# Fetching experts head by head from the first head on, with the memory values moved under the fetches

## The chip, the cores and the metric

One core of one Trainium2 chip runs the whole program in one launch. The time is device microseconds of that core. The core has TensorE (PE), VectorE (DVE), ScalarE (ACT), GpSimd (POOL) and SyncE (SP, which here only issues DMAs), each with its own instruction queue, and 16 DMA engines.

## The reference

Two transformer blocks over 256 tokens of width 1024. Block 1: attention and retention, `w_out`, then a layer of 16384 experts of which each token takes 8 heads x 16; block 2: SSD and latent attention, attention to 256 memory tokens, a convolutional feed-forward layer. What matters here is the expert layer:

```python
q = (xb @ w_query).reshape(tb, 8, 2, 128)
s = einsum('thpd,hpnd->thpn', q, sub_keys)          # 2 x 128 scores per token and head
top_s, top_i = top_k(s, 16)
cand = top_s[:, :, 0, :, None] + top_s[:, :, 1, None, :]
best_s, pos = top_k(cand, 16);  gate = softmax(best_s)
u = expert_down[eid];  act = gelu(einsum('thkd,td->thk', u, xb))
out = einsum('thk,thkd->td', gate * act, expert_up[eid])
```

and, of memory attention in block 2, `k = mem_h @ wk` and `v = mem_h @ wv`, which depend on nothing but the memory tokens.

## The kernel before, in words

The tokens are two tiles of 128, one token per partition. All products with weights are made of three passes (`mm3`, L173 to L175) on a high and a low half: `piece` (L148) loads 512 KB of a weight (`raw`, SP), rounds it on ScalarE (`wh`, L167) and takes the rest on VectorE (`wl`, L168). The pool of these tiles has three buffers of each.

Block 1 (`mix1`) runs attention (`diff_*`), retention (`ret_*`), scaling, transposes (`to_T`, L223) and `w_out`. Between its steps `fill(n)` draws pieces of work from a generator, to keep TensorE busy while other engines work: first the projections `rqk`, `rv`, `rg`, then `memory_values`, that is eight pieces of `w_mem_v` and eight of `w_mem_k`, whose results go to DRAM (`memkv`). What is left over after block 1 is handed on as `self.memory`.

`queries` (L606) multiplies by 16 pieces of `w_query`, two per head, and makes the scores `sS` of four (head, half) pairs at a time. `picks` and `choose` (L631) find the 16 best of 128, twice, and the 16 best sums, for four heads of one tile at once, so four units in all; every step is on VectorE, and the generators yield an estimate of their cost, by which `picking` spreads them over other work. The first unit is done while the queries are still running.

`experts` (L688) then goes through 2 tiles x 128 slots. A slot is one indirect DMA (L767, GpSimd's queue) that brings for each of the 128 tokens one row of 8 KB, 1 MB in all, into one of eight buffers `uv`: 1024 numbers of `expert_down` and 1024 of `expert_up`. VectorE takes the dot product with the normed token (`junk`, L770, result in `dots`), ScalarE the gelu of a pair of slots (L773), VectorE writes for each slot a diagonal matrix of gate times gelu (`dg`, L779), and TensorE multiplies the diagonal with the second half of the row and sums all slots of a tile in PSUM (L783, four rows in the trace per slot). The next fetch into that buffer waits for these. Under tile 0 run the other units of the choice and the memory values left over; between the tiles `joined` adds the sum to the residual `xr`. Block 2 follows.

The order on each engine is that of the program text, as far as a scheduler in the compiler doesn't interleave the independent strands.

Of the kernel before, what the change touches and what calls it, by code (L numbers as in the profile page):

```python
# [8 lines left out]
F32 = mybir.dt.float32  # L9
# [105 lines left out]
class K:  # L115
    def __init__(self, tc, I, out, dbg):
        self.tc, self.nc, self.I, self.out, self.dbg = tc, tc.nc, I, out, dbg


# [28 lines left out]
    def piece(self, src, shape, between=None):  # L148
# [3 lines left out]
        def t(tag, dt):  # L152
            x = self.wp.tile([128, 1024], dt, name=tag, tag=tag)
# [8 lines left out]
        for i in range(shape[0] if between else 1):  # L162
# [5 lines left out]
            self.wl = nc.vector.tensor_sub(lo[:, s], raw[:, s], h[:, s])  # L168
# [140 lines left out]
    def mix1(self):  # L309
# [3 lines left out]
        with self.tc.tile_pool(name="m1", bufs=1, reuse_waits="tile") as mp:  # L313
# [184 lines left out]
            fill(2)  # L498
            a = diff_turn(p)
            p = diff_scores(2)  # L500
            w = ret_scores(0)
# [3 lines left out]
            ret_out(0, w)  # L505
            w = ret_scores(1)
            fill(1)
# [4 lines left out]
            ret_out(1, w)  # L512
            w = ret_scores(2)
            fill(2)
            a = diff_turn(p)
            ret_out(2, w)
            w = ret_scores(3)
# [10 lines left out]
            fill(2)  # L528
            self.to_T([blk(h) for h in range(4)], [dg] * 4, mT[0], mT[1], 0)
            fill(2)  # L530
# [22 lines left out]
            fill(1)  # L553
# [6 lines left out]
            self.memory = fill  # L560
# [47 lines left out]
    def queries(self, pool, skT, sS):  # L608
# [4 lines left out]
        for b in range(16):  # L613
            if b < 2:
                o = two[b]
            else:
                o = self.pa([128, 256])
                self.proj_T(self.hT, self.piece(I["w_query"][b], [8, 128]), 8, o)
            if b == 2:
                self.r = self.res_r()  # L620
            if b % 4 == 0:
                qT = pool.tile([128, 4, 256], F32, name="qT", tag="qT", bufs=2)
            nc.scalar.activation(qT[:, b % 4], o, AF.Copy)
            if b % 4 == 3:
                q = b // 4
                for t in range(2):
                    s = self.pb([128, 4, 128])
                    for i in range(4):
                        nc.tensor.matmul(s[:, i], qT[:, i, t * 128:(t + 1) * 128], skT[:, 4 * q + i],
                                         start=True, stop=True)  # L630
                    nc.scalar.activation(sS[t][q], s, AF.Copy, scale=self.r[:, t:t + 1])  # L631
            yield

    def choose(self, t, hf, vals, idx, P):

        nc = self.nc
        H = 4
        hs = slice(4 * hf, 4 * hf + 4)
# [9 lines left out]
        yield 700  # L648
        yield from self.extract([cand[:, i] for i in range(H)], [cs[:, i] for i in range(H)],
                                [best[:, i] for i in range(H)], [pos[:, i] for i in range(H)], 610)  # L650
# [7 lines left out]
        yield 450  # L658
# [13 lines left out]
        yield 900  # L672
        io = self.io16[:, None, None, :].to_broadcast([128, H, 16, 16])
        ij = P([2, H, 16], "rij")
        for s in range(2):
            eq = P([H, 16, 16], "eq", F16)
            nc.vector.tensor_tensor(eq, ab[:, s, :, :, None].to_broadcast([128, H, 16, 16]), io, op=OP.is_equal)  # L677
            yield 1130
            nc.vector.tensor_mul(eq, eq, ix[:, s, :, None, :].to_broadcast([128, H, 16, 16]))
            yield 600  # L680
# [3 lines left out]
            yield 870  # L684
# [3 lines left out]
    def experts(self):  # L688


        nc, I = self.nc, self.I
        with self.tc.tile_pool(name="p2", bufs=1, reuse_waits="tile") as p2:
# [8 lines left out]
            sS = [[P([4, 128], f"sS{t}{q}") for q in range(4)] for t in range(2)]  # L701
# [4 lines left out]
            mr = [P([4, 128], f"mr{t}") for t in range(2)]  # L706
            gf = P([1024], "gf")
            nc.sync.dma_start(gf, I["ffn_gr"].to_broadcast([128, 1024]))
            self.fg = P([1024], "fgr")
            nc.sync.dma_start(self.fg, I["final_g"].to_broadcast([128, 1024]))  # L710
            self.xg = [P([512], f"xg{t}") for t in range(2)]
            xn = [P([1024], f"xn{t}") for t in range(2)]

            def picks(t, hf):
                for q in (2 * hf, 2 * hf + 1):
                    yield from self.extract([sS[t][q][:, i] for i in range(4)], [mr[t][:, i] for i in range(4)],
                                            [vals[t][:, 4 * q + i] for i in range(4)],
                                            [idx[t][:, 4 * q + i] for i in range(4)], 810)
                yield from self.choose(t, hf, vals, idx, P)

            pick = [picks(t, hf) for t in range(2) for hf in range(2)]
            debt = [0]

            def picking(time, upto):

                debt[0] += time
                while debt[0] > 0:
                    while pick and len(pick) > 4 - upto:
                        cost = next(pick[0], None)
                        if cost is not None:  # L730
                            debt[0] -= cost
                            break
                        pick.pop(0)
                    else:
                        debt[0] = 0

            with self.tc.tile_pool(name="qp", bufs=1, reuse_waits="tile") as qp:
                skT = qp.tile([128, 16, 128], F32, name="skT")
                nc.sync.dma_start(skT, I["skT"])
                for b, _ in enumerate(self.queries(qp, skT, sS)):  # L740
                    if b == 3:
                        for t in range(2):
# [904 lines left out]
```

## Time and profile before

| | us |
|---|---|
| three runs | 1355.0, 1357.12, 1356.94 (median 1356.94) |
| profiled execution | 1354.52 |
| its span | 1352.6 |
| first fetch issued | 203.91 |
| last dot product begins | 880.62 |
| TensorE clock granted, mean | 0.981 |

The span is the time from the first instruction to the last; the stages follow each other: block 1 to 147.3, queries to 203.9, experts to 880.7, block 2 to the end. A busy share is an average over them, so the windows by stage are what counts.

### The profile page before, as it was taken

How to read it: one execution, taken by the hardware profiler on the slowest of the kernel's cores; microseconds unless marked ns; L12 is line 12 of the kernel's file. 1: busy time of each engine (PE TensorE's matmuls, PEld its weight loads, DVE VectorE, ACT ScalarE, POOL GpSimd, SP SyncE). 2: the span in 40 equal slices, each digit the busy share in tenths (PEclk: the TensorE clock that was granted, in tenths of full speed). 3: DMA queues.
4: the chain of work that ended last, by engine and by line, in shares of the span. 5: the costliest groups of instructions: out<-in, count | busy, mean ns of one | idle time of the engine just before them, and what ended most of it. 6: DMA issues, size and time to landing. Idle time of an engine off the chain costs nothing.

```text
span 1352.6 us, 16359 instructions
## 1 busy us (share of the span) xinstructions
PE 1158.9 (86%) x5430; PEld 792.1 (59%) x5430; DVE 997.2 (74%) x2334; ACT 489.1 (36%) x969; POOL 291.2 (22%) x280
## 2 busy tenths in 40 slices
PE   8999997668777777787777777789999999999996
PEld 6888996323223222332232222269997898999996
DVE  6877798997666666666656666678996886988887
ACT  6676653210000000100000000056878574755554
POOL 0010104335333334344343343210001000000001
PEclk9999998879999999999999999999999999999999
DMA  7636749899999999899999999936434364556562
GB/s 262 232 120 203 225 150 382 359 352 386 422 422 421 422 421 422 342 423 421 421 421 423 421 422 421 395 101 190 141 106 129 112 231 126 190 187 188 187 185 96
DMA packets 81655, 388.07 MB, mean 287 GB/s; under 512 B 8292, under 2 KB 10404, under 8 KB 48548
## 3 DMA queue, kind: packets, MB, share of 16 engines
q0 software_dynamic: 36864, 268.45, 48.2%
q1 hardware_dynamic: 42692, 115.96, 26.7%
q10 hardware_dynamic: 2016, 2.62, 0.5%
q8 instruction: 43, 0.70, 0.2%
q14 instruction: 40, 0.33, 0.1%
HBM read 383.86 MB, written 3.15 MB: 286 GB/s over the span
## 4 chain that ended last, share of the span: by engine, by line
PE 41%; DMA 23%; issue 13%; DVE 10%; POOL 6%; ACT 1%; POOLq 0%; DVEq 0%; ACTq 0%
DMA uv<-in_uv_dram,eid 23%; POOL uv L767 6%; PE pa L173 6%; PE pa L174 6%; PE pa L175 6%; PE pa L1476 4%; PE pb L173 4%; PE pb L174 4%; PE pb L175 4%; DVE junk L770 2%; DVE wl L168 1%; PE pb L783 1%; PE pb L1060 1%; DVE dg L779 1%; DVE eq L677 1%
## 5 line engine op out<-in xcount | busy, mean ns | idle before, releaser
L783 PE MATMUL pb<-uv,dg 128*128 128x512 f32 x1024 | 486.6, 620 | 168.5 <-DVE dg L779 160.0
L783 PEld LDWEIGHTS pb<-uv,dg 128*128 128x128 f32 x1024 | 190.3, 195 | 460.9 <-DVE dg L779 257.2
L770 DVE SCALAR_TENSOR_TENSOR junk<-uv,xn 128x1024 bf16<-128x1024 f32 x256 | 313.4, 1224 | 166.2 <-DMA uv<-in_uv_dram,eid 159.6
L767 POOL DMA_INDIRECT uv<-in_uv_dram,eid x256 | 260.4, 1017 | 431.7 <-PE pb L783 327.7
L168 DVE TENSOR_TENSOR wl<-raw,wh 128x1024 fp32r<-128x1024 f32 (+3 forms) x203 | 248.8, 1228 | 70.7 <-ACT wh L167 66.8
L167 ACT ACTIVATE wh<-raw 128x1024 fp32r<-128x1024 f32 (+3 forms) x203 | 212.1, 1047 | 196.5 <-PE pa L174 39.5
L773 ACT ACTIVATE dots<-dots,rs_y 128x2 f32<-128x2 f32 x128 | 37.8, 295 | 578.5 <-DVE junk L770 578.1
L173 PE MATMUL pb<-nTh,wh 128*128 128x256 f32 x416 | 117.7, 283 | 0.0
L174 PE MATMUL pb<-nTl,wh 128*128 128x256 f32 x416 | 117.7, 283 | 0.0
L175 PE MATMUL pb<-nTh,wl 128*128 128x256 f32 x416 | 117.4, 283 | 0.0
L779 DVE TENSOR_SCALAR dg<-cvt,dots,gate 128x128 f32<-128x128 f32 x256 | 78.0, 394 | 51.5 <-ACT dots L773 51.5
L174 PEld LDWEIGHTS pb<-nTl,wh 128*128 128x128 f32 x416 | 79.5, 191 | 1.0
L173 PEld LDWEIGHTS pb<-nTh,wh 128*128 128x128 f32 x416 | 79.5, 191 | 1.0
L175 PEld LDWEIGHTS pb<-nTh,wl 128*128 128x128 f32 x416 | 79.5, 191 | 0.0
L173 PE MATMUL pa<-nTh,wh 128*128 128x256 f32 x256 | 74.1, 289 | 0.0
L1500 POOL TENSOR_TENSOR xs<-xr,ng 128x512 f32<-128x512 f32 x4 | 5.1, 1294 | 313.9 <-DVE xr L1498 313.9
L175 PE MATMUL pa<-nTh,wl 128*128 128x256 f32 x256 | 72.5, 283 | 0.0
L174 PE MATMUL pa<-nTl,wh 128*128 128x256 f32 x256 | 72.4, 283 | 0.0
L173 PE MATMUL pa<-wh,nTh 128*128 128x512 f32 (+1 forms) x144 | 58.1, 412 | 8.2 <-ACT wh L167 7.1
L174 PE MATMUL pa<-wl,nTh 128*128 128x512 f32 (+1 forms) x144 | 57.6, 400 | 1.7 <-DVE wl L168 1.6
L175 PE MATMUL pa<-wh,nTl 128*128 128x512 f32 (+1 forms) x144 | 56.7, 394 | 0.0
L173 PEld LDWEIGHTS pa<-nTh,wh 128*128 128x128 f32 x256 | 48.9, 191 | 1.1 <-issue 1.0
(455 smaller groups left out, 1797.5 us busy)
## 6 DMA issues: line engine op xcount, KB each, us to landing
raw<-in_w_ffn_up_dram SPq DMA_DIRECT2D x44, 512.0 KB, 3.6
raw<-in_w_out_dram SPq DMA_DIRECT2D x24, 512.0 KB, 3.7
raw<-in_w_in_dram SPq DMA_DIRECT2D x23, 512.0 KB, 4.7
raw<-in_w_ffn_down_dram SPq DMA_DIRECT2D x22, 512.0 KB, 3.6
raw<-in_w_query_dram SPq DMA_DIRECT2D x16, 512.0 KB, 3.6
raw<-in_w_xbc_dram SPq DMA_DIRECT2D x16, 512.0 KB, 4.3
raw<-in_w_mem_v_dram SPq DMA_DIRECT2D x8, 512.0 KB, 4.7
raw<-in_w_mem_k_dram SPq DMA_DIRECT2D x8, 512.0 KB, 6.2
```

The source lines that it names most:

```text
L167: nc.scalar.activation(h[:, s], raw[:, s], AF.Copy)
L168: self.wl = nc.vector.tensor_sub(lo[:, s], raw[:, s], h[:, s])
L173: mm(out, a[0], b[0], start=start, stop=False)
L174: mm(out, a[0], b[1], start=False, stop=False)
L175: mm(out, a[1], b[0], start=False, stop=stop)
L677: nc.vector.tensor_tensor(eq, ab[:, s, :, :, None].to_broadcast([128, H, 16, 16]), io, op=OP.is_equal)
L767: nc.gpsimd.indirect_dma_start(x, None, I["uv"], bass.IndirectOffsetOnAxis(ap=eids[:, s + i:s + i + 1], axis=0))
L770: nc.vector.scalar_tensor_tensor(junk, x[:, :1024], 1.0, xn[t], op0=OP.mult, op1=OP.mult, accum_out=dots[:, i:i + 1])
L773: nc.scalar.activation(dots, dots, AF.Gelu, scale=self.r[:, t:t + 1])
L779: nc.vector.tensor_scalar(dg[:, i], self.ident, ds[:, i:i + 1], gates[:, s0 + i:s0 + i + 1], op0=OP.mult, op1=OP.mult)
L783: nc.tensor.matmul(acc[d], dg[:, i], rs[i][:, 1024 + 512 * d:1536 + 512 * d], start=s0 + i == 0, stop=s0 + i == 127)
L1476: nc.tensor.matmul(acc[d][t], a[x][:, t * 128:(t + 1) * 128], w[y][:, d], start=b == 0 and x + y == 0, stop=b == 21 and x == 1)
```

## The change

1. `memory_values` leaves the fillers of block 1. It is drawn piece by piece under tile 0's fetches, from slot 58 on. Some retention steps move to where its pieces stood.
2. Queries, scores and choices go head by head. Units of choice: head 0 of tile 0, head 1, then pairs of heads, then the two units of four heads of tile 1. The fetches begin when head 0 is chosen; the rest of the queries and choices runs under them.
3. The raw query tiles have a pool of their own (`qraw`, four buffers).
4. The low halves `wl` are taken on GpSimd from the third query piece to the end of the memory values.
5. Six `uv` buffers until slot 56, then eight.
6. `dg` moves to ScalarE; the gate is multiplied into `dots` before it by a small VectorE product. Of four slots one (`sl % 4 == 2`) has no `dg` and no matmul: VectorE multiplies and adds its row into `xr` (64 of 256 slots).
7. `xn` takes its gains by DMA and is multiplied in place.

```diff
...
+            pool = self.rawp if tag == "raw" and self.rawp else self.wp
+            x = pool.tile([128, 1024], dt, name=tag, tag=tag)
...
-            self.wl = nc.vector.tensor_sub(lo[:, s], raw[:, s], h[:, s])
+            self.wl = self.low_by.tensor_sub(lo[:, s], raw[:, s], h[:, s])
...
                 for name in ("rqk", "rv", "rg"):
                     yield from block(name)
-                yield from self.memory_values(*memory)
...
             diff_out(3, a)
-            ret_out(3, w)
             ds = ds.rearrange("p t h -> p (t h)")
             nc.vector.tensor_scalar(ds, ds, 1.0 / 128, EPS, op0=OP.mult, op1=OP.add)
             r = self.rsqrt(ds, 8)
+            ret_out(1, w)
+            w = ret_scores(2)
             for t in range(2):
                 for h in range(4):
                     nc.scalar.activation(mix[:, t, h * 128:(h + 1) * 128], dif[:, t, h], AF.Copy,
                                          scale=r[:, 4 * t + h:4 * t + h + 1])
-            fill(2)
+            w3 = ret_scores(3)
+            ret_out(2, w)
+            ret_out(3, w3)
+            fill.rest()
             self.to_T([blk(h) for h in range(4)], [dg] * 4, mT[0], mT[1], 0)
-            fill(2)
             vv = self.sm([128, 8], F32, "bvv", 1)
             nc.vector.tensor_scalar(vv, mv[:, :, :, 1].rearrange("p t h -> p (t h)"), EPS, None, op0=OP.add)
             rr = self.rsqrt(vv, 8)
...
             self.to_T([blk(4 + h) for h in range(4)], [self.pv("ret_g", h) for h in range(4)], mT[0], mT[1], 4)
-            fill(1)
...
-            self.memory = fill
+            self.memory = Filler(self.memory_values(*memory))
...
+        self.r = self.res_r()
+        for h in range(8):
+            qT = pool.tile([128, 2, 256], F32, name="qT", tag="qT", bufs=2)
+            for i in range(2):
+                o = two[i]
+                if h:
+                    o = self.pa([128, 256])
+                    self.proj_T(self.hT, self.piece(I["w_query"][2 * h + i], [8, 128]), 8, o)
+                nc.scalar.activation(qT[:, i], o, AF.Copy)
+                if h and not i:
+                    yield
+            for t in range(2):
+                s = self.pb([128, 2, 128])
+                for i in range(2):
+                    nc.tensor.matmul(s[:, i], qT[:, i, t * 128:(t + 1) * 128], skT[:, 2 * h + i], start=True, stop=True)
+                nc.scalar.activation(sS[t][h], s, AF.Copy, scale=self.r[:, t:t + 1])
+    def choose(self, t, h0, H, vals, idx, P):
...
+            for t in range(2):
+                nc.sync.dma_start(xn[t], I["ffn_gr"].to_broadcast([128, 1024]))
...
+            units = [(0, 0, 1), (0, 1, 1)] + [(0, h, 2) for h in (2, 4, 6)] + [(1, 0, 4), (1, 4, 4)]
...
+            uvs = [up] * 6
+            count = [0]
+
+            def fetch(t, acc):
+
+                gates = self.gate[t].rearrange("p h k -> p (h k)")
+                eids = self.eid[t].rearrange("p h k -> p (h k)")
+                last = None
+                for s in range(0, 130, 2):
+                    new = None
+                    if s < 128:
+                        rows = []
+                        dots = up.tile([128, 2], F32, name="dots", tag="dots", bufs=4)
+                        for i in range(2):
+                            pool = uvs[count[0] % len(uvs)]
+                            count[0] += 1
+                            x = pool.tile([128, 2048], F32, name="uv", tag="uv", bufs=uvs.count(pool))
+                            nc.gpsimd.indirect_dma_start(x, None, I["uv"],
+                                                         bass.IndirectOffsetOnAxis(ap=eids[:, s + i:s + i + 1], axis=0))
+                            junk = self.junk([128, 1024], "junk", BF)
+                            nc.vector.scalar_tensor_tensor(junk, x[:, :1024], 1.0, xn[t], op0=OP.mult, op1=OP.mult,
+                                                           accum_out=dots[:, i:i + 1])
+                            rows.append(x)
+                        nc.scalar.activation(dots, dots, AF.Gelu, scale=self.r[:, t:t + 1])
+                        nc.vector.tensor_mul(dots, dots, gates[:, s:s + 2])
+                        new = s, rows, dots
+                    if last:
+                        s0, rs, ds = last
+                        dg = up.tile([128, 2, 128], F32, name="dg", tag="dg", bufs=3)
+                        for i in range(2):
+                            sl = s0 + i
+                            if sl % 4 == 2:
+                                nc.vector.scalar_tensor_tensor(self.xr[:, t], rs[i][:, 1024:], ds[:, i:i + 1],
+                                                               self.xr[:, t], op0=OP.mult, op1=OP.add)
+                                continue
+                            nc.scalar.activation(dg[:, i], self.ident, AF.Copy, scale=ds[:, i:i + 1])
+                            for d in range(2):
+                                nc.tensor.matmul(acc[d], dg[:, i], rs[i][:, 1024 + 512 * d:1536 + 512 * d],
+                                                 start=sl == 0, stop=sl == 127)
+                    last = new
+                    yield s
+
+            two = lambda: [self.pb([128, 512]) for _ in range(2)]
+            with self.tc.tile_pool(name="qp", bufs=1, reuse_waits="tile") as qp:
+                skT = qp.tile([128, 16, 128], F32, name="skT")
+                nc.sync.dma_start(skT, I["skT"])
+                with self.tc.tile_pool(name="qraw", bufs=4) as self.rawp:
+                    query = Filler(self.queries(qp, skT, sS))
+                    query(1)
+                    nc.gpsimd.tensor_mul(xn[0], xn[0], self.xr[:, 0])
+                    self.low_by = nc.gpsimd
+                    query(2)
+                    picking(1e6, 0, 1)
+                    acc = two()
+                    tile0 = fetch(0, acc)
+                    for s in tile0:
+                        if s == 2:
+                            nc.gpsimd.tensor_mul(xn[1], xn[1], self.xr[:, 1])
+                        if s % 4 == 2:
+                            query(1)
+                        done = min(8, 2 + (s + 2) // 8)
+                        picking(1400, 0, done)
+                        if s in (12, 28):
+                            picking(1e6, 0, 2 if s == 12 else 4)
+                        if s == 54:
+                            break
+                    query.rest()
+                self.rawp = None
+            with self.tc.tile_pool(name="up2", bufs=1, reuse_waits="tile") as up2:
+                uvs += [up2] * 2
+                self.fg = up2.tile([128, 1024], F32, name="fgr")
+                nc.sync.dma_start(self.fg, I["final_g"].to_broadcast([128, 1024]))
+                self.xg = [up2.tile([128, 512], F32, name=f"xg{t}") for t in range(2)]
+                for s in tile0:
+                    if s % 4 == 2:
+                        self.memory(1)
+                    picking(1400, 1, 8)
+                    if s % 32 == 26:
+                        picking(1e6, 0, min(8, 2 * (s // 32) + 4))
+                self.memory.rest()
+                self.low_by = nc.vector
+                picking(1e6, 1, 8)
+                self.hT = (self.nt.tile([128, 8, 256], F32R, name="nTh", tag="nTh"),
+                           self.nt.tile([128, 8, 256], F32R, name="nTl", tag="nTl"))
+                for d in range(2):
+                    self.joined(0, d, acc[d], gg)
+                acc = two()
+                for s in fetch(1, acc):
...
...
```

The DMA queue of SP at the end of block 1, before (`w_mem_v`, `w_mem_k` are the memory values):

```order
L166 DMA raw<-in_w_mem_v_dram 128x2x512 x8
L166 DMA raw<-in_w_out_dram 128x2x512 x4
L166 DMA raw<-in_w_mem_k_dram 128x1024
L166 DMA raw<-in_w_out_dram 128x2x512 x4
L166 DMA raw<-in_w_query_dram 128x1024 x5
L699 DMA iota<-in_cv_dram 128x16
L708 DMA gf<-in_ffn_gr_dram 128x1024
L710 DMA fgr<-in_final_g_dram 128x1024
L739 DMA skT<-in_skT_dram 128x2048
L166 DMA raw<-in_w_query_dram 128x1024 x11
L166 DMA raw<-in_w_mem_k_dram 128x1024 x7
```

and of the change:

```order
L169 DMA raw<-in_w_out_dram 128x2x512 x8
L169 DMA raw<-in_w_mem_v_dram 128x2x512 x3
L695 DMA iota<-in_cv_dram 128x16
L705 DMA xn_1380<-in_ffn_gr_dram 128x1024
L705 DMA xn_1381<-in_ffn_gr_dram 128x1024
L781 DMA skT<-in_skT_dram 128x2048
L169 DMA raw<-in_w_query_dram 128x1024 x16
L807 DMA fgr<-in_final_g_dram 128x1024
L169 DMA raw<-in_w_mem_v_dram 128x2x512 x5
L169 DMA raw<-in_w_mem_k_dram 128x1024 x8
```

All `w_query` loads now stand behind three loads of the values and in one run; the others of the values come behind them.

GpSimd's queue from the normed tokens `xn` to the fetches, before:

```order
L743 TENSOR_TENSOR xn_1569<-xr,gf 128x1024
L743 TENSOR_TENSOR xn_1570<-xr,gf 128x1024
L767 DMA uv<-in_uv_dram,eid_1559 128x2048 x128
L767 DMA uv<-in_uv_dram,eid_1560 128x2048 x3
L828 TENSOR_TENSOR xg_1567<-xr,fgr 128x512
```

and of the change:

```order
L785 TENSOR_TENSOR xn_1380<-xn_1380,xr 128x1024
L793 TENSOR_TENSOR xn_1381<-xn_1381,xr 128x1024
L171 TENSOR_TENSOR wl<-raw,wh 128x1024 x5
L753 DMA uv<-in_uv_dram,eid_1376 128x2048 x16
L171 TENSOR_TENSOR wl<-raw,wh 128x1024
L753 DMA uv<-in_uv_dram,eid_1376 128x2048 x4
```

Five low halves stand ahead of the first fetch, and one more behind each four fetches after the first 16.

TensorE at the first turn of `mix` (L223, now L226), before:

```order
L174 MATMUL pa<-wl,memTh 128x512
L175 MATMUL pa<-wh,memTl 128x512
L173 MATMUL pa<-wh,memTh 128x512
L223 MATMUL pb<-cvt,mix 128x128
L174 MATMUL pa<-wl,memTh 128x512
L223 MATMUL pb<-cvt,mix 128x128 x2
L175 MATMUL pa<-wh,memTl 128x512
L223 MATMUL pb<-cvt,mix 128x128
L173 MATMUL pa<-wh,memTh 128x512
L223 MATMUL pb<-cvt,mix 128x128
```

and of the change (`rqk` and `rw` are retention's scores and weights):

```order
L178 MATMUL pb<-rqkTh,rqkTl 128x256
L176 MATMUL pb<-rqkTh 128x256
L177 MATMUL pb<-rqkTl,rqkTh 128x256
L178 MATMUL pb<-rqkTh,rqkTl 128x256
L481 MATMUL pb<-rv,rw 128x128 x8
L226 MATMUL pb<-cvt,mix 128x128 x8
L176 MATMUL pa<-wh,mTh 128x512
L177 MATMUL pa<-wl,mTh 128x512
L176 MATMUL pa<-wh,mTh 128x512
L178 MATMUL pa<-wh,mTl 128x512
```

The turn stood among matmuls of the values (`memTh`); now it stands between retention and `w_out` (`mTh`).

## Rows read from the trace of the kernel before

**Rows 1.** The page: gigabytes per second that the DMA moved, in 40 slices of 33.8 us.
```profile
GB/s 262 232 120 203 225 150 382 359 352 386 422 422 421 422 421 422 342 423 421 421 421 423 421 422 421 395 101 190 141 106 129 112 231 126 190 187 188 187 185 96
```

**Rows 2.** Stretches: length, busy time (instructions) of each engine, granted clock, DMA share, GB/s.
```profile
147.30:203.90 56.60, 55.97 (x468) 55.47 (x467) 52.71 (x217) 31.55 (x51) 6.03 (x2) 1.00 0.59 187
203.90:880.70 676.80, 506.03 (x1200) 211.62 (x1199) 454.68 (x1098) 61.24 (x167) 262.94 (x258) 0.97 0.99 405
225.00:310.00 85.00, 62.10 (x171) 29.95 (x170) 84.65 (x329) 15.90 (x28) 31.15 (x25) 0.85 0.92 359
310.00:406.60 96.60, 73.70 (x161) 28.67 (x160) 62.21 (x124) 5.91 (x20) 40.05 (x42) 1.00 1.01 418
406.60:555.00 148.40, 111.50 (x239) 43.56 (x239) 90.49 (x177) 8.57 (x29) 55.76 (x57) 0.99 1.01 421
555.00:590.00 35.00, 28.81 (x75) 13.58 (x74) 21.90 (x46) 6.83 (x22) 17.88 (x16) 0.90 0.87 346
590.00:880.70 290.70, 216.18 (x466) 84.06 (x465) 178.07 (x349) 17.14 (x58) 108.62 (x112) 0.99 1.00 416
```

**Rows 3.** TensorE groups, 60 to 147.3 us: count, busy us, mean ns, idle before.
```profile
L173 PE MATMUL pa<-wh,memTh 128*128 128x512 f32 x32 | 13.1, 410 | 0.0
```

**Rows 4.** Timeline of 109 to 117 us: start, length, engine, line, operation, count.
```profile
109.58 0.14 DVE L522 TENSOR_SCALAR dss<-dss 128x8 f32<-128x8 f32 x1
...
115.25 1.85 ACT L526 ACTIVATE mix<-mix,rs_y 128x128 f32<-128x128 f32 x6
...
115.25 0.40 PE L175 MATMUL pa<-wh,memTl 128*128 128x512 f32 x1
115.48 0.40 PE L173 MATMUL pa<-wh,memTh 128*128 128x512 f32 x1
115.72 0.30 PE L223 MATMUL pb<-cvt,mix 128*128 128x128 f32 x1
```

**Rows 5.** Timeline: the first query loads on SP, the first fetch on GpSimd.
```profile
134.16 12.22 SPq L166 DMA_DIRECT2D raw<-in_w_query_dram  x5
...
203.91 1.15 POOL L767 DMA_INDIRECT uv<-in_uv_dram,eid  x1 [43.57 <-DVE vals L602]
```

**Rows 6.** Timeline of GpSimd and VectorE, 153 to 161 us.
```profile
154.31 6.03 POOL L743 TENSOR_TENSOR xn<-xr,gf 128x1024 f32<-128x1024 f32 x2 [67.41 <-DVE rs_y L199]
...
153.50 1.23 DVE L168 TENSOR_TENSOR wl<-raw,wh 128x1024 fp32r<-128x1024 f32 x1
154.95 3.15 DVE L168 TENSOR_TENSOR wl<-raw,wh 128x1024 fp32r<-128x1024 f32 x1 [0.22 <-ACT wh L167]
```

**Rows 7.** DMA issues: KB each, median us from issue to landing.
```profile
raw<-in_w_query_dram SPq DMA_DIRECT2D x16, 512.0 KB, 3.6
...
uv<-in_uv_dram,eid POOLq DMA_INDIRECT x256, 13.0
```

**Rows 8.** Timeline of the steady loop, one pair of rows.
```profile
702.49 3.70 PE L783 MATMUL pb<-uv,dg 128*128 128x512 f32 x8 [1.35 <-DVE dg L779]
...
704.75 0.94 POOL L767 DMA_INDIRECT uv<-in_uv_dram,eid  x1 [2.36 <-PE pb L783]
```

**Rows 9.** Groups between 225 and 310 us.
```profile
L770 DVE SCALAR_TENSOR_TENSOR junk<-uv,xn 128x1024 bf16<-128x1024 f32 x25 | 30.4, 1215 | 0.0
...
L779 DVE TENSOR_SCALAR dg<-cvt,dots,gate 128x128 f32<-128x128 f32 x26 | 7.7, 344 | 0.3 <-ACT dots L773 0.3
...
L168 DVE TENSOR_TENSOR wl<-raw,wh 128x864 fp32r<-128x864 f32 (+1 forms) x5 | 5.6, 1111 | 0.0
```

**Rows 10.** Timeline of TensorE after two gaps.
```profile
255.23 1.12 PE L783 MATMUL pb<-uv,dg 128*128 128x512 f32 x2 [2.60 <-DVE dg L779]
...
282.78 2.07 PE L783 MATMUL pb<-uv,dg 128*128 128x512 f32 x2 [3.25 <-DVE dg L779]
```

**Rows 11.** Stretches at these gaps: TensorE busy, granted clock, DMA share, GB/s.
```profile
255.00:260.00 5.00, 3.70 (x8) 1.00 1.01 423
280.00:285.00 5.00, 2.22 (x3) 0.67 1.00 415
```

More of the change, by code (lines that the diff above doesn't have):

```diff
@@ L504, in mix1 @@
             diff_out(1, a)
-            ret_out(0, w)
-            w = ret_scores(1)
-            fill(1)
+            w = ret_scores(0)
             a = diff_turn(p)
@@ L612, in queries @@
         self.first_T([I["w_query"][b] for b in range(2)], two, self.pv("ffn_g", 0, 8))
[L613 to L631, printed above, removed]
+        self.r = self.res_r()
[14 more added lines that the diff above has]
+                nc.scalar.activation(sS[t][h], s, AF.Copy, scale=self.r[:, t:t + 1])
             yield
-    def choose(self, t, hf, vals, idx, P):
+    def choose(self, t, h0, H, vals, idx, P):
         nc = self.nc
-        H = 4
-        hs = slice(4 * hf, 4 * hf + 4)
+        hs = slice(h0, h0 + H)
         v = vals[t].rearrange("p (h s) k -> p h s k", s=2)[:, hs]
@@ L691, in experts @@
         nc, I = self.nc, self.I
-        with self.tc.tile_pool(name="p2", bufs=1, reuse_waits="tile") as p2:
+        with self.tc.tile_pool(name="p2", bufs=1, reuse_waits="tile") as p2, \
+                self.tc.tile_pool(name="up", bufs=1, reuse_waits="tile") as up:
             def P(shape, tag, dt=F32, bufs=1):
@@ L700, in experts @@
             nc.vector.tensor_copy(self.io16, iota)
-            sS = [[P([4, 128], f"sS{t}{q}") for q in range(4)] for t in range(2)]
+            sS = [[P([2, 128], f"sS{t}{h}") for h in range(8)] for t in range(2)]
             vals = [P([16, 16], f"vals{t}") for t in range(2)]
@@ L722, in experts, with picking @@
+            units = [(0, 0, 1), (0, 1, 1)] + [(0, h, 2) for h in (2, 4, 6)] + [(1, 0, 4), (1, 4, 4)]
+            pick = [(u, picks(*u)) for u in units]
             debt = [0]
-            def picking(time, upto):
+            def picking(time, t, h):
                 debt[0] += time
                 while debt[0] > 0:
[L728 to L732, printed above, removed]
+                    if not pick or (pick[0][0][0], pick[0][0][1] + pick[0][0][2]) > (t, h):
+                        debt[0] = 0
+                        break
+                    cost = next(pick[0][1], None)
+                    if cost is None:
@@ L733, in picking @@
                         pick.pop(0)
                     else:
[L735 to L742, printed above, removed]
-                            nc.gpsimd.tensor_mul(xn[t], self.xr[:, t], gf)
-                    if b >= 8:
-                        picking(2000, 1)
-                picking(1e6, 1)
+                        debt[0] -= cost
@@ new lines, in experts @@
+            with self.tc.tile_pool(name="up2", bufs=1, reuse_waits="tile") as up2:
[18 more added lines that the diff above has]
+                for s in fetch(1, acc):
+                    if s == 112:
+                        ws = [self.piece(I["w_latq"][k], [2, 432]) for k in range(3)]
+                    elif s == 120:
+                        A = [self.pa([128, 512]) for _ in range(2)]
+                        self.latents(ws, 0, A[0])
+                for d in range(2):
+                    self.joined(1, d, acc[d], gg)
+                self.latents(ws, 1, A[1])
+                ws.append(self.piece(I["w_latq"][3], [2, 432]))
+                for u in range(2):
+                    self.latents(ws, u, A[u], (3,))
```

106 lines of the change are left out of this document (20 added, 86 removed).

## Prediction

> **What bounds the kernel now.** I read the page's gigabytes per second first: from the seventh slice to the 26th the DMA moves 340 to 423, outside them mostly 100 to 260 [rows 1]. So the expert stage, half of the span, is the stage in which the memory system is the limit, and the windows by stage say how tight that limit is. From the first fetch (203.91, [rows 5]) to the end of the last one at 880.7 the DMA is 99% busy and moves 405 GB/s over 676.8 us, which is 274.1 MB; in its undisturbed stretch, 406.6 to 555, it moves 421 [rows 2]. At 421 the same bytes take 651 us: 25.7 us are lost, and the table shows where: 359 GB/s from 225 to 310 (85 x 62 / 421 = 12.5 us lost) and 346 from 555 to 590, the join of the two tiles (35 x 75 / 421 = 6.2). A fetched slot is 1.049 MB, 2.49 us at 421 GB/s.
>
> From 225 to 310 VectorE is the limit: 84.65 us busy of 85 [rows 2], 25 dot products of 1.215 us, 7.7 us of `dg`, 5.6 of low halves [rows 9], and the rest, some 40 us, mostly choosing. 25 slots in 85 us are 3.4 us a slot, against 2.49.
>
> Before the first fetch TensorE is the limit: 55.97 of the 56.6 us of the query stage, clock 1.00 [rows 2]. So there are three levers: the moment of the first fetch, the bytes moved after it, and the slots at which something other than the DMA sets the pace.
>
> **The change part by part.** I count from the profiled execution, 1354.5 us, of which 1352.6 are the span; the median of the runs is 1356.9, 2.4 more, and I add those at the end.
>
> *Block 1.* The memory values leave it: three groups of 32 matmuls on the value matrix (one of them in [rows 3]), which follow each other at 0.23 us [rows 4], 96 x 0.227 = 21.8 us, and one key piece, 24 matmuls of half the columns, 2.8 us: 24.6 us of TensorE. But they were cover. The sum of squares is scaled at 109.58, the scaled `mix` comes at 115.25, the transpose at 115.72 [rows 4]: 6.1 us in which TensorE had 26 or so of those matmuls to run. Now two retention heads stand there, and the last `ret_out` ends just ahead of the transposes. I take 9 us of new gaps (bounds 3, if the retention covers most of the chain, and 18, if every such chain is bare), and 3 us for the clock that falls after a gap: behind one of 2.60 us it held 1.00, behind one of 3.25 us it was 0.67 over five microseconds [rows 10, 11]. Block 1 ends 12 to 13 us earlier, near 134.5 for 147.3.
>
> *First fetch.* Before, the first query loads were issued at 134.16 [rows 5], 13 us ahead of their use. Now their buffers lie in memory that block 1 uses to its end, so the first is issued about 2.6 us after the last `w_out` matmul, lands 3.6 us later [rows 7] and is rounded in 1.1: TensorE stands some 8 us. Two pieces (2.9 us each by the row count and pitch) and head 0's scores end 17 us after block 1. Head 0's choice is about 45 short VectorE instructions; in 225 to 310 some two units of four heads cost 40 us, 5 us a head where four share an instruction, so one alone is between 5 and 20; I take 8.5, nearer the low end. On GpSimd the two products `xn` and five low halves come ahead of the fetches; the two products took 6.03 us [rows 6], so five more at 2.3 to 3.4 end at about the same time as the choice. The first fetch is at 134.5 + 26 = 160 (bounds 152 and 170), 44 us earlier.
>
> *Bytes.* After the first fetch now come 9 or 10 query pieces (5 MB; the low halves of the others stand ahead of it), 13 memory pieces (6.8) for seven before (3.7), and the writes of the values (some 1 MB more): about 283 MB for 274, 22 us at 421 GB/s.
>
> *Slots 0 to 67.* VectorE per four slots: four dots of 1.22 and, new, one 128x1024 sum. That operation isn't in the trace; the dot, same shape and two such inputs, took 1.215 [rows 9], a residual addition of half that width would make it 1.4, and I take 1.25 (at 1.4 it adds 0.15 x 64 = 10 us of VectorE, hidden wherever the DMA is late). Two gate products of 0.1 us are added, `dg` (0.3 each at its pace) goes to ScalarE, which was busy 61 us of 677 [rows 2] and covers it. Sum 6.3 us, under the DMA's 9.96. On top comes the choosing left over, about 80 us; by the order of the instructions some 6 us of it stand in slots 0 to 3, 17 in slots 4 to 31, and 58 in slots 32 to 67. So: slots 0 to 3 about 7 us beyond landing; slots 4 to 31 are DMA-bound, 28 x 2.49 + 6 x 1.24 (a query piece of 512 KB) = 77.2, and with two crowded places 82; slots 32 to 67 take VectorE 9 x 6.3 + 58 = 115 for a DMA need of 97.
>
> *Low halves on GpSimd.* 26 of them now run between fetches. In the trace a low half on VectorE took 3.15 us beside the product `xn` on GpSimd, 1.23 just ahead of it, and the GpSimd product 3.0 [rows 6]. So each can hold VectorE for 1.9 us. Where the DMA is the limit that is hidden; the nine in slots 32 to 67 are not: 0 to 9 x 3.0 = 27 us, nearest row 17, and I take 10, as VectorE's many small operations there have one large input or less. The Trainium skill ("SBUF — State Buffer", the section on SBUF's two separate sides) says that VectorE and GpSimd share a port pair as an exclusive lock, held for the whole instruction, for a VectorE operation with two SBUF inputs against a GpSimd operation that reads SBUF, and that the loser fully blocks. The trace agrees (3.15 for 1.23); by the rule alone every dot that meets a low half waits for its end, and the sum would lose the 27.
>
> Slots 0 to 67 then take 7 + 82 + 115 + 10 = 214 us, and slot 68 stands near 374, before 406.6. Slots 68 to 127 are DMA-bound: 60 x 2.49 = 149.4, 13 pieces 16, writes 5: 171 us, end of tile 0 at 545 for 555. In that stage GpSimd's own queue isn't late: four issues of about 1 us and a low half of 3 in 10 us.
>
> *Six buffers.* With eight, a fetch lands 13.0 us after its issue [rows 7], most of it waiting behind others; TensorE's four rows and the issue of the next fetch into a buffer 2.26 us after their start [rows 8] close the loop. Six buffers give 6 x 2.49 = 15 us per turn. That is just enough by these rows (5.5 us for the least landing, 4 for the pair's second dot and gelu, 4.5 to the reissue); above it each microsecond costs a sixth per slot. I take nothing beyond the 4 us above; bounds 0 and 0.9 us a slot, which is what 225 to 310 showed over the 2.49.
>
> *Tile 1, join and the rest.* 6.3 us of VectorE and 12 matmul rows of 0.43 (5.2 us) per 9.96 us of DMA: as before, 325.7 us [rows 2]. All told 10 us earlier: 1344.5, against the median 1347.
>
> **Rivals.** (a) *The DMA never waits:* the choosing and the locks fit between the landings, so from the first landing on the stage lasts 283 MB / 421 = 672 us and the 6 of the join. For it: 418 GB/s from 310 to 406.6 with VectorE 62 of 96.6 busy [rows 2]. Against it: 225 to 310. It ends at 160 + 7 + 678 = 845 for 880.7: 1319 profiled, 1321 as a median.
>
> (b) *Slower: the early slots go at VectorE's and the ring's pace.* Place: slots 0 to 67; mechanism: six buffers, choosing and the held port pair make each slot cost 3.4 us, as in 225 to 310 [rows 2, 9]. 7 + 68 x 3.4 = 238 us, slot 68 at 398, tile 0 ends at 569: 14 later, 1368 profiled, 1371. It decides from 3.2 us a slot on (160 + 7 + 68 x 3.2 = 384, 10 over mine). For it: that stretch had eight buffers and still lost. Against: per four slots VectorE has less to do than there.
>
> (c) *The clock.* With one row in four off TensorE, its gaps in the steady loop alternate near 1.5 and 3.3 us, and 3.25 is where the clock fell [rows 10, 11]. At half clock 12 rows take 10.3 us against 9.96: up to 0.34 x 32 = 11 us in a tile, which eats the gain: 1357. Against: at that pace the gaps close, and the clock comes back.
>
> (d) *Block 1 gains nothing:* every chain is bare; it ends at 141, the gain is 3 to 4 us: 1353.
>
> **How the numbers follow.** Chances: my forecast (gain of 4 to 20 us) 0.44, (a) 0.18, (b) 0.24, (c) 0.08, (d) 0.06. The likeliest is 1347, its own range 1337 to 1353. A measurement here can tell 0.2%, 2.7 us. Faster: the forecast, (a) and most of (d) less the cases near zero, 0.62; same 0.10 from the edges of forecast and (c), (d); slower 0.28, (b) and part of (c). From 1321, the whole of (a), to 1366, most of (b): 8 in 10.
>
> **What would show it.** The first fetch between 152 and 170 and the last `w_out` matmul near 134; slots 4 to 31 at 2.8 to 3.0 us each with the DMA above 0.95, slots 32 to 67 at 3.2 to 3.5 with VectorE over 0.95; dots of 2 to 4 us beside low halves on GpSimd; slot 68 between 365 and 385; tile 1 at 2.49 a slot with TensorE about 52% busy at clock 1.00. A first fetch after 175, slots 4 to 31 above 3.3 with a VectorE that idles (the ring), or a granted clock below 0.9 in tile 1 would prove me wrong.

## The result, and the profile after

The changed kernel takes 1389.6 us (median of 4 runs, 1387.2 to 1397.7) against 1356.0: a ratio of 1.026, 95% interval 1.022 to 1.030. It is slower, where 1347 and "faster" were forecast. The profiled execution took 1397.7, the longest of the four; its span is 1395.8.

The page, TensorE's granted clock in tenths and gigabytes per second, 40 slices of 34.9 us:

```profile
PEclk9999878888778989988889888999999999999998
...
GB/s 254 232 93 136 207 382 359 299 307 294 287 328 347 411 405 399 422 342 421 421 422 421 422 421 420 423 201 177 146 128 103 109 226 145 176 194 184 184 185 100
```

Against [rows 1] the transfers begin one slice earlier, but the slices from the eighth to the 13th show 287 to 347 GB/s, where before they showed 352 to 422. Six stretches (length, busy time of PE, PEld, DVE, ACT, POOL, then clock, DMA share, GB/s): from just behind block 1 to the first fetch, slots 0 to 31, slots 32 to 67, slots 68 to 127, the join, tile 1.

```profile
139.60:170.00 30.40, 22.83 (x170) 22.41 (x170) 20.61 (x87) 15.38 (x26) 15.49 (x8) 0.83 0.64 207
170.00:284.10 114.10, 80.79 (x270) 44.55 (x269) 83.20 (x250) 29.25 (x67) 55.55 (x43) 0.82 0.90 345
284.10:424.60 140.50, 86.78 (x240) 44.60 (x239) 127.63 (x448) 35.08 (x71) 60.34 (x43) 0.78 0.79 296
424.60:597.00 172.40, 134.90 (x438) 74.03 (x438) 122.73 (x166) 43.13 (x99) 100.18 (x69) 0.89 1.00 404
597.00:640.00 43.00, 31.88 (x72) 13.89 (x70) 28.26 (x52) 11.01 (x34) 22.28 (x19) 0.85 0.88 356
640.00:923.40 283.40, 188.66 (x339) 72.98 (x340) 182.59 (x311) 47.90 (x142) 130.46 (x110) 0.88 1.00 417
```

To be read against [rows 2]. The DMA share is 0.90 and 0.79 in the first 68 slots, and VectorE busy 127.6 of 140.5 us in the second stretch. Tile 1 moves its bytes at 417 GB/s as before, with TensorE at a clock of 0.88. The stages in us, from the starts of dot products and fetches:

| | forecast | measured | kernel before |
|---|---|---|---|
| last `w_out` matmul | 134.5 | 138.2 | 147.3 |
| first fetch | 160 | 170.0 | 203.9 |
| slot 4 | 167 | 187.1 | 230.0 |
| slots 4 to 31, each | 2.9 | 3.46 | 3.13 |
| slots 32 to 67, each | 3.5 | 3.90 | 2.47 |
| slot 68 | 374 | 424.6 | 406.7 |
| slots 68 to 127, together | 171 | 172.4 | 148.3 |
| last dot product | 870 | 923.4 | 880.6 |

The start, in a timeline of TensorE, SP and GpSimd (start, length, idle before and its releaser), which answers to [rows 4, 5]:

```profile
87.75 0.58 PE L427 MATMUL pb<-dkTh,dqTh 64*128 64x256 f32 x1 [4.47 <-ACT mix L461]
...
109.91 2.53 PE L226 MATMUL pb<-cvt,mix 128*128 128x128 f32 x8 [3.16 <-ACT mix L523]
...
146.73 0.58 PE L176 MATMUL pa<-nTh,wh 128*128 128x256 f32 x1 [7.10 <-ACT wh L170]
...
139.84 3.13 SPq L169 DMA_DIRECT2D raw<-in_w_query_dram  x4
...
169.99 1.14 POOL L753 DMA_INDIRECT uv<-in_uv_dram,eid  x1 [2.86 <-DVE eid L679]
```

Block 1 has two bare gaps, 4.47 and 3.16 us; the query loads go out at 139.84, and TensorE stands 7.10 us. Then a low half on GpSimd (297.63) and VectorE beside it, which answers to [rows 6]:

```profile
297.63 2.38 POOL L171 TENSOR_TENSOR wl<-raw,wh 128x1024 fp32r<-128x1024 f32 x1
...
297.15 3.42 DVE L671 TENSOR_TENSOR eq<-rab,io 128x512 f16<-128x512 f16 x1
300.49 0.15 DVE L760 TENSOR_TENSOR dots<-dots,gate 128x2 f32<-128x2 f32 x1
```

An `eq` product that elsewhere takes 0.70 us ends half a microsecond after the low half. The groups of VectorE between 170 and 424.6 show what was held:

```profile
L756 DVE SCALAR_TENSOR_TENSOR junk<-uv,xn 128x1024 bf16<-128x1024 f32 x68 | 90.0, 1323 | 9.8 <-DMA uv<-in_uv_dram,eid 9.5
...
L659 DVE TENSOR_SCALAR rg<-rf 128x32 f32<-128x32 f32 x3 | 3.3, 1085 | 0.0
...
L659 DVE TENSOR_SCALAR rg<-rf 128x64 f32<-128x64 f32 x2 | 0.4, 184 | 0.0
```

The dots are at 1.32 for 1.215 [rows 9]. And a one-input operation on 32 numbers per token (`rg`) has a mean of 1.085 us in one form and 0.184 in a wider one, as one of its three took 2.93 beside the low half at 236.75: being small or having one input did not spare it. The searches of the choice were spared. They ran beside low halves at their usual 0.28 us:

```profile
155.18 4.76 POOL L171 TENSOR_TENSOR wl<-raw,wh 128x1024 fp32r<-128x1024 f32 x2 [3.39 <-ACT wh L170]
...
158.89 0.28 DVE L597 MATCH_REPLACE8 mr<-vals,sS 128x128 f32<-128x128 f32 x1
```

Over the whole tile I compared each VectorE instruction that overlaps one of the 25 low halves after the first fetch with the median of its own kind: 19 of the 25 met one, most of them lost 2.0 to 2.9 us, 48.4 in all: 7.7 in slots 4 to 31, 13.9 in 32 to 67, 26.8 behind. VectorE's waits in the first 68 slots (in total, times, longest):

```profile
DVE vals L591 <- ACT sS L626: 22.7, 6, 6.0
DVE dots L760 <- ACT dots L759: 9.8, 16, 4.4
DVE junk L756 <- DMA uv<-in_uv_dram,eid: 9.5, 8, 2.3
```

The first is new: VectorE stands 22.7 us at the first maximum of a choice, for scores that come late. What holds them up stands in TensorE's longest wait over the same stretch, and in the lines around VectorE's longest single one:

```profile
PE pb L773 <- ACT dg L771: 82.7, 22, 8.4
...
328.52 2.39 POOL L171 TENSOR_TENSOR wl<-raw,wh 128x1024 fp32r<-128x1024 f32 x1
...
335.69 5.40 PE L773 MATMUL pb<-uv,dg 128*128 128x512 f32 x8 [3.61 <-ACT dg L771]
340.52 0.69 PE L178 MATMUL pa<-nTh,wl 128*128 128x256 f32 x1
...
345.47 0.49 DVE L591 MAX8 vals<-sS 128x8 f32<-128x128 f32 x2 [6.02 <-ACT sS L626]
345.88 1.21 DVE L756 SCALAR_TENSOR_TENSOR junk<-uv,xn 128x1024 bf16<-128x1024 f32 x1
```

A low half stands in GpSimd's queue behind every four fetches, and in TensorE's queue the products of a query piece stand among the rows of the slots in the same way. No wait of TensorE in these slots is put down to a low half. The low half ends at 330.91; the pass that reads it (L178) begins at 340.52, behind eight rows that waited for `dg`, and for the other pieces after the first fetch that distance is 4 to 15 us. So VectorE stands for scores, the scores wait for slot rows ahead of them in TensorE's queue, and those rows for `dg`, which comes from VectorE's dots. The last query product ends at 343.7.

### The profile page after: what moved, and what is told of

The parts are those of the page before. It is cut to its first block, busy times and chain, and to the rows that moved or that the text cites. A ratio compares the mean times of both kernels' runs of the same rounds, so it can differ in the third digit from the quotient of the medians.

```text
span 1395.8 us, 15825 instructions
## 1 busy us (share of the span) xinstructions
PE 1125.7 (81%) x5174; PEld 780.7 (56%) x5174; DVE 1044.9 (75%) x2321; ACT 565.8 (41%) x1176; POOL 409.2 (29%) x310
## 4 chain that ended last, share of the span: by engine, by line
PE 42%; DVE 19%; issue 13%; DMA 9%; POOL 8%; ACT 3%; POOLq 0%; ACTq 0%; DVEq 0%
DMA uv<-in_uv_dram,eid 8%; POOL uv L753 7%; DVE junk L756 7%; PE pb L773 6%; PE pa L176 5%; PE pa L177 5%; PE pa L178 5%; PE pa L1504 4%; PE pb L176 4%; PE pb L177 4%; PE pb L178 4%; DVE dots L760 2%; DVE xr L768 1%; DVE eq L671 1%; PE pb L1088 1%
## 5 line engine op out<-in xcount | busy, mean ns | idle before, releaser
L773 PE MATMUL pb<-uv,dg 128*128 128x512 f32 x768 | 446.9, 734 | 224.8 <-ACT dg L771 224.8
L773 PEld LDWEIGHTS pb<-uv,dg 128*128 128x128 f32 x768 | 170.3, 233 | 470.0 <-ACT dg L771 288.8
L756 DVE SCALAR_TENSOR_TENSOR junk<-uv,xn 128x1024 bf16<-128x1024 f32 x256 | 331.6, 1295 | 106.6 <-DMA uv<-in_uv_dram,eid 105.1
L753 POOL DMA_INDIRECT uv<-in_uv_dram,eid x256 | 305.3, 1193 | 361.8 <-PE pb L773 220.8
L171 DVE TENSOR_TENSOR wl<-raw,wh 128x1024 fp32r<-128x1024 f32 (+3 forms) x173 | 210.3, 1219 | 72.9 <-ACT wh L170 72.3
L178 PE MATMUL pb<-nTh,wl 128*128 128x256 f32 x416 | 117.4, 283 | 0.0
L771 ACT ACTIVATE dg<-cvt,dots 128x128 f32<-128x128 f32 x192 | 70.1, 396 | 71.2 <-DVE dots L760 71.2
L760 DVE TENSOR_TENSOR dots<-dots,gate 128x2 f32<-128x2 f32 x128 | 40.8, 318 | 71.7 <-ACT dots L759 71.7
L768 DVE SCALAR_TENSOR_TENSOR xr<-uv,dots,xr 128x1024 f32<-128x1024 f32 x64 | 85.0, 1328 | 2.0
L178 PEld LDWEIGHTS pb<-nTh,wl 128*128 128x128 f32 x416 | 79.5, 191 | 0.0
L178 PE MATMUL pa<-nTh,wl 128*128 128x256 f32 x256 | 77.2, 301 | 0.5 <-DVE wl L171 0.5
L171 POOL TENSOR_TENSOR wl<-raw,wh 128x1024 fp32r<-128x1024 f32 x30 | 73.0, 2436 | 12.5 <-ACT wh L170 12.0
```

Source lines behind the costliest of these rows:

```text
L171: self.wl = self.low_by.tensor_sub(lo[:, s], raw[:, s], h[:, s])
L178: mm(out, a[1], b[0], start=False, stop=stop)
L753: nc.gpsimd.indirect_dma_start(x, None, I["uv"], bass.IndirectOffsetOnAxis(ap=eids[:, s + i:s + i + 1], axis=0))
L756: nc.vector.scalar_tensor_tensor(junk, x[:, :1024], 1.0, xn[t], op0=OP.mult, op1=OP.mult, accum_out=dots[:, i:i + 1])
L760: nc.vector.tensor_mul(dots, dots, gates[:, s:s + 2])
L768: nc.vector.scalar_tensor_tensor(self.xr[:, t], rs[i][:, 1024:], ds[:, i:i + 1], self.xr[:, t], op0=OP.mult, op1=OP.add)
```

## The experiments

All times are medians; each kernel's runs stand beside runs of the kernel before, whose medians were 1354.8 to 1357.3.

**Low halves on VectorE.** `-  self.low_by = nc.gpsimd` (the line taken out).

> The change with all low halves on VectorE again (none on GpSimd). Theory 'ring' (six buffers, each held longer than 15 us, set the pace of slots 0 to 67): the low halves add 26 x 1.2 us to VectorE and free GpSimd's queue, slots 0 to 67 stay at 3.5 to 3.8 us, time within 8 us of the change's 1389.6. Theory 'lock' (GpSimd's low halves hold VectorE, 3.42 us for an eq product of 0.70): slots 0 to 67 fall to 3.3 us or less, 20 us or more faster (1370 or less).

1360.9 (1359.0 to 1364.1): 28.7 us less, by far the largest of the single edits. But slots 4 to 67 did not fall to 3.3 us: they took 3.65 (4 to 31) and 3.37 (32 to 67). They hold more work: with the engine of the low halves as the only edit, the last query product ends at 237.3 us for 343.7, and the memory values are done by slot 54 for 120. Slot 68 comes 8.1 us earlier; most of the gain sits in slots 68 to 127 (2.48 us each for 2.92). It needed splitting, below.

**Query tiles in the common pool; then eight buffers.** `-  with self.tc.tile_pool(name="qraw", bufs=4) as self.rawp:`; and `-  uvs = [up] * 6  +  uvs = [up] * 8`.

> The change with the raw query tiles in the common pool of three instead of their own four that reuse block 1's memory; still six uv buffers. Both theories of the fetch stage: the pace of slots 0 to 67 stays near 3.66 us. Only the first query loads go out before the end of block 1, so TensorE's 7.1 us stand after the last w_out matmul shrinks to 1 to 2 us, the first fetch comes at 163 to 165 for 170, and the time falls by 4 to 7 us.

> As e2_no_qraw, and the memory that is freed holds two more uv buffers: eight from the first fetch on. Theory 'ring': slots 4 to 31 go from 3.46 us to 2.8 or less, slots 32 to 67 from 3.9 to 3.4 (VectorE-bound), 25 to 40 us faster than e2_no_qraw. Theory 'lock' or VectorE's load alone: less than 10 us faster than e2_no_qraw, as the buffers would only wait longer for VectorE.

1385.0 and 1376.4 (1371.6 to 1385.9). The first removes TensorE's 7.1 us and has head 0's scores 4 us earlier (153.6 for 157.9), yet the first fetch is at 170.6: the choice takes 16.5 us for 12.0, beside four low halves and a product on GpSimd. The earlier fetch that I expected failed. The second gains 8.6, with 2.85 us in slots 4 to 31 (3.06 without) and 3.86 in slots 32 to 67: less than theory "ring" said, and not where the time is. The two ratios, 1.020 to 1.023 and 1.012 to 1.022, overlap, so the 8.6 is barely clear of noise.

**Six buffers in the kernel before.** `-  bufs=8  +  bufs=6` at L766.

> The kernel before with six uv buffers instead of eight, nothing else. Theory 'ring': the stretch with choosing (225 to 310) gets slower than 3.4 us a slot, and even the undisturbed slots of tile 1 rise over 2.49, 15 to 40 us slower in all. Theory 'lock': six buffers suffice for a turn of 15 us, less than 8 us slower.

1367.9, 13 us slower, a ratio of 1.010 (1.008 to 1.012), between what the two theories expect. Landing time, and tile 1:

```profile
uv<-in_uv_dram,eid POOLq DMA_INDIRECT x256, 8.6
...
600.00:892.00 292.00, 216.67 (x463) 84.49 (x463) 177.54 (x348) 17.14 (x58) 113.23 (x113) 0.99 1.00 415
```

A fetch lands after 8.6 us for 13.0 [rows 7]: two buffers less are mostly, as I read it, less waiting behind others; 2.52 us a slot in tile 1 for 2.48.

**Both, and all slots on TensorE.** e1 and e3 together; then also `-  if sl % 4 == 2:  +  if sl < 0:`.

> e3_ring8 (eight buffers, query tiles in the common pool) and e1_low_on_dve (low halves on VectorE) together. If the ring's and the lock's costs add, 1389.6 - 28.7 - 13.2 = 1347.7. If both are one cost (a buffer is held long because VectorE is held), the second edit adds little to the first: 1355 to 1361.

> e6_ring8_low_dve with every slot on TensorE again (no row summed on VectorE). VectorE loses 64 x 1.33 = 85 us, some 45 of them in tile 0, where slots 4 to 67 were VectorE-bound: theory 'VectorE's load sets the pace there' expects 10 to 25 us less than e6. Theory 'TensorE at half clock sets it' expects no gain or a loss, since TensorE gets a third more rows, unless the clock stays up.

1364.4 and 1358.9. With the low halves on VectorE, eight buffers and the common pool gain nothing (3.5 us more than e1, above both expectations). So I read the ring's 8.6 us as a consequence: buffers were kept long because VectorE was late. Taking the sums off VectorE gains 5.5, less than the 10 to 25 expected.

**All slots on TensorE in the change itself.** The same edit alone.

> The change with every slot on TensorE again (the 64 sums on VectorE undone), low halves still on GpSimd, six buffers. Theory 'lock and VectorE's load': VectorE loses 85 us, 22 of them in slots 0 to 67, and one large two-input operation in five that a low half can stop: 10 to 25 us faster than 1389.6. Theory 'TensorE's clock': its gaps shrink by a third more rows, the granted clock returns from 0.88 to 0.97 or more in tile 1, where the DMA is the limit, and nothing is gained there; a gain, if any, comes before slot 68.

1383.7, 5.9 less, under the 10 to 25 of its first theory. Tile 1 (columns as above):

```profile
620.00:906.00 286.00, 213.00 (x461) 82.92 (x462) 151.09 (x287) 56.53 (x172) 104.42 (x110) 1.00 1.01 419
```

Its clock is 1.00 for 0.88, and a slot takes 2.47 us for 2.49: the fallen clock was real, and together with the sums on VectorE, which the same edit takes away, it cost tile 1 some 2 us.

**Held without data: a product, and a memset.** e1 plus one GpSimd instruction behind every fourth fetch of tile 0: `+  nc.gpsimd.tensor_sub(scr, xn[0], hist[-4][:, 0:1].to_broadcast([128, 1024]))`, or `+  nc.gpsimd.memset(scr, 0.0)` with a ScalarE copy of one column that paces it.

> e1_low_on_dve (all low halves on VectorE) with 30 added GpSimd products of 128x1024 that nobody needs, one behind every fourth fetch of tile 0, of data that are ready by then. Theory 'lock': each holds VectorE's two-input operations and, 2.4 us long, gives back most of what e1 had gained: 15 to 30 us slower than e1's 1360.9, with VectorE operations of 2 to 4 us beside them. Theory 'order' (e1 gained because the memory values no longer stand in the queue of fetches): within 6 us of e1.

> As e7_dummy_tt, but the 30 added GpSimd instructions are memsets of the same 128x1024 tile, which read nothing. If the lock needs a GpSimd operation that reads the on-chip memory, as the skill says, VectorE keeps its pace and the time stays within 5 us of e1's 1360.9, a memset's own length in GpSimd's queue apart; if any long GpSimd instruction delays the fetches or VectorE, it comes out like e7_dummy_tt.

1379.6 and 1368.0. GpSimd's added instruction and VectorE's dots, of the product, then of the memset (count, busy, mean ns, idle before):

```profile
L779 POOL TENSOR_TENSOR scr<-xn,dots 128x1024 bf16<-128x1024 f32 x29 | 56.8, 1959 | 0.8 <-issue 0.2
...
L758 DVE SCALAR_TENSOR_TENSOR junk<-uv,xn 128x1024 bf16<-128x1024 f32 x121 | 170.4, 1408 | 32.2 <-DMA uv<-in_uv_dram,eid 31.7
```

```profile
L779 POOL MEMSET scr<- 128x1024 bf16 x29 | 28.0, 964 | 6.5 <-ACT tiny L780 6.5
...
L758 DVE SCALAR_TENSOR_TENSOR junk<-uv,xn 128x1024 bf16<-128x1024 f32 x126 | 154.0, 1222 | 58.5 <-DMA uv<-in_uv_dram,eid 58.4
```

Beside products the dots take 1.41 us, beside memsets 1.22, as alone. VectorE lost 43.6 us to the 30 products and 0.2 to the memsets by the count used above. That shows the hold, and that a product holds VectorE where a memset does not; that the reading makes the difference is likely but not separated from the length (1.96 us for 0.96). In the kernel with products VectorE has no wait for scores, so a hold alone does not make that wait. The memset kernel is 7.2 us slower than e1 all the same, where 5 were expected besides the memset's own length; its place in GpSimd's queue and the copy on ScalarE are candidates, which I did not separate.

**GpSimd for the queries only, or for the memory values only.** `self.low_by` set back, or set, at slot 56.

> The change with GpSimd's low halves for the query pieces alone; those of the memory values are on VectorE. Of the 28.7 us by which e1_low_on_dve is under the change, theory 'lock' (a held VectorE costs where VectorE sets the pace, before slot 68) puts most on the query pieces: 1375 to 1385 here. Theory 'order' (the memory values, tied to GpSimd's queue of fetches, come late and their bytes fall into the DMA-bound slots 68 to 127) puts it on the memory pieces: 1360 to 1370 here.

> The other half: GpSimd's low halves for the memory values alone, those of the queries on VectorE. Theory 'lock': 1362 to 1372, with slots 4 to 67 as in e1_low_on_dve. Theory 'order': 1378 to 1390, with slots 68 to 127 at 2.8 us or more, as in the change.

1374.9 and 1371.1: the queries' low halves cost 14.0 over e1, the memory values' 10.2. By the times both runs lie at or in the ranges of theory "lock". But the 14.0 us are not the hold alone: in e12 VectorE lost 13.0 us to its nine low halves by the count used above and waited 15.4 us for scores. And slots 68 to 127 of e13 take 2.92 us each, as theory "order" said. In e13 slots 0 to 31, 32 to 67 and 68 to 127, and VectorE's waits to slot 68:

```profile
170.80:291.00 120.20, 85.12 (x368) 53.16 (x367) 113.95 (x476) 43.63 (x86) 40.73 (x35) 0.89 0.85 324
291.00:396.40 105.40, 68.93 (x131) 29.03 (x130) 89.58 (x218) 19.90 (x50) 57.41 (x41) 0.83 0.95 376
396.40:568.60 172.20, 136.46 (x440) 74.92 (x439) 122.97 (x165) 42.83 (x99) 103.14 (x70) 0.88 1.02 417
```

```profile
DVE junk L756 <- DMA uv<-in_uv_dram,eid: 17.0, 18, 3.1
DVE dots L760 <- ACT dots L759: 4.4, 12, 0.4
```

No wait for scores is left (the last query product ends at 239.5), and slot 68 comes at 396.4 for 424.6, though VectorE does eight low halves itself. These two traces are 29 us apart and the medians 18.5, so a part of the 28 belongs to the execution that was profiled. In slots 68 to 127 VectorE was held 27 us more, and no cost of it shows: 172.2 us at 417 GB/s, as forecast for the bytes alone.

**Memory values back in block 1**, in the change, and in e9.

> The change with the memory values back among block 1's fillers (block 1 exactly as in the kernel before); all else as in the change. Block 1 ends near 147 for 138, the first fetch comes 8 to 9 us later; nine of 13 memory pieces, their writes and nine of GpSimd's low halves leave tile 0: 9 x 1.24 + 4 = 15 us of DMA if it is the limit there, and up to 9 x 3 us of held VectorE. Sum: 5 to 30 us faster than 1389.6. If the move under the fetches was free, as its cover was meant to be, 8 us slower.

> e9_ring8_low_dve_all_pe with the memory values back among block 1's fillers: only the queries and choices head by head, the early first fetch, and dg on ScalarE are left of the change. Block 1 costs 9 us more, tile 0 loses 9 pieces and their writes (15 us of DMA) and 9 x 1.2 us of VectorE. If the stage is bound by bytes and VectorE as I now read it: 5 to 15 us under e9's 1358.9, that is 1344 to 1354, at or below the kernel before. If the early fetches are worth nothing in any form: 1358 or more.

1387.1 (1379.7 to 1390.9) and 1351.2. In the change the move is worth nothing clear of noise either way: block 1 is 9.8 us longer, and tile 0, from the first fetch to slot 127, 20.3 shorter, in traces that are 11 us apart where the medians are 2.5. In e9 undoing it gains 7.6, and e10 beats the kernel before: 0.9955 (0.994 to 0.997). Its query start, slots 0 to 31, 32 to 67, 68 to 127:

```profile
148.00:176.30 28.30, 25.64 (x197) 24.82 (x195) 26.07 (x111) 15.23 (x28) 4.82 (x3) 0.94 0.57 183
176.30:291.00 114.70, 95.79 (x443) 63.86 (x444) 96.33 (x406) 44.64 (x90) 39.41 (x32) 0.90 0.88 351
291.00:405.50 114.50, 88.84 (x252) 41.52 (x251) 86.42 (x276) 30.07 (x75) 47.51 (x42) 0.96 1.00 393
405.50:552.90 147.40, 109.89 (x239) 42.82 (x240) 77.47 (x148) 28.81 (x88) 54.70 (x57) 1.00 1.01 421
```

It fetches 27.7 us before the kernel before and starts slot 127 only 2.1 us before it (these two traces differ by less than 1 us in all, the medians by 6): slots 0 to 31 share VectorE (96.3 of 114.7) and TensorE with the query pieces.

**dg and the gate back on VectorE**, in e10.

> e10_best_mem_in_block1 with dg and the gate back on VectorE, as in the kernel before: then only the order (queries and choices head by head, early first fetch) is left of the change. VectorE gets 256 x 0.3 us more and loses 128 gate products of 0.15; ScalarE loses 256 x 0.35. If VectorE sets the pace of slots 4 to 31 there: 5 to 12 us slower than e10's 1351.2. If ScalarE's queue (dg and gelu behind the roundings) does: equal or up to 5 us faster.

1351.4, ratio 0.9958 (0.994 to 0.997): no difference from e10. Where dg runs doesn't matter here.

## Why the prediction was wrong

*Block 1 and the first fetch: the mechanism right, 10 us too early.* The gaps and the falling clock took 15.5 us of the 24.6 for my 12; TensorE took 8.8 us for the first two pieces after standing 7.1, for 5.8; head 0's choice took 12.0 us for 8.5.

*Slots 0 to 3: a slip of 10.* I put "7 us beyond landing" for them into the sum as if it were their whole time; from the first fetch to slot 4 were 17.1.

*The failing step is "Low halves on GpSimd".* Slot 68 came 50.6 us after its forecast: 10 by the first fetch, 10 by the slip, 15 in slots 4 to 31 and 15.5 in slots 32 to 67. For the low halves I had put 10 us into that sum, in slots 32 to 67 alone, "as VectorE's many small operations there have one large input or less". They cost VectorE 44 us: 13.9 held in that stretch (7 low halves), 7.7 held in slots 4 to 31, which I had called hidden, and 22.7 waiting for scores, which I put at nothing. The searches were spared, but products of two numbers and the one-input operation above were held for the length of a low half. By the Trainium skill's rule ("SBUF — State Buffer", the section on SBUF's two separate sides) the sum would have lost 27, I said. The trace agrees in that a dot that meets a low half is held (by 2.0 to 2.8 us), but the hold in that stretch alone, 13.9, was nearer to my 10. And the order that I had shown myself, one low half behind every four fetches, I priced as GpSimd's own time only ("GpSimd's own queue isn't late"). What hangs on it is the chain of product, scores and choice, which then stands between the slots on TensorE too, and VectorE stood 22.7 us at its end. Taking hold and wait away for the queries (e13) brings slot 68 28 us forward between these two traces: VectorE then has eight low halves to do (10 us) and waits 7.5 us more for landings. How much of the time the hold costs there and how much the wait, no run separates.

*Slots 4 to 31 "DMA-bound": wrong*, 3.46 us each for 2.9, as I read it by the same two causes; six buffers had a part, as e3 shows (2.85 for 3.06). *Slots 32 to 67: 140.5 us for 125.* VectorE was busy 127.6 of them, 13.9 of it held, so its own load was rightly sized (114 for 115).

*Slots 68 to 127, tile 1, join: right* (172.4 for 171; the held VectorE is hidden there).

*Six buffers: "I take nothing".* 13 us in the kernel before, 8.6 between e2 and e3, nothing seen with the low halves on VectorE (e6 against e1). A pair of this stage with TensorE at a granted clock of 0.57 (289.9 to 296.4), and a fetch that stood 7.88 us, by the profile for a VectorE instruction:

```profile
289.93 6.44 PE L773 MATMUL pb<-uv,dg 128*128 128x512 f32 x8 [5.47 <-ACT dg L771]
...
293.98 0.94 POOL L753 DMA_INDIRECT uv<-in_uv_dram,eid  x1 [7.88 <-DVE rab L663]
```

*Rivals.* (b) came nearest: slower, in slots 0 to 67, above 3.2 us a slot, by VectorE, its hold and its wait for scores; little of its ring was left with the low halves on VectorE. (c): the clock did fall to 0.88 in tile 1, with no loss beyond 2 us. (a) and (d) fell.

*The early fetch itself* is worth far less than the 44 us I let it bring forward: even with nearly everything else undone, 27.7 us earlier at the first fetch are 2 at the end of tile 0. The engines' work that filled 147 to 204 still has to be done beside the dots.

## What to carry to other kernels

An operation moved to an idle engine takes two things along: what it holds that the busy engine needs, and its place in that engine's queue, to which the steps behind it are tied on the other engines too. Price the second by following who waits for its result, to the engine whose time decides; here it was the very engine that the move was to relieve. And a stage that starts earlier is worth only the spare time of the engines that then have to share it.

## What was not expected of the hardware

A GpSimd product of 128x1024 (2.4 us) stopped VectorE products of any size, down to two numbers per token (2.86 us), and a one-input operation on 32 (2.93 us for some 0.2). The searches MAX8, FIND_INDEX8 and MATCH_REPLACE8 ran beside it at 0.28 us as usual. A GpSimd memset of the same tile (0.96 us) stopped no VectorE operation.
